# A store in a top-2 dispatch kernel moves from the sync queue to the scalar queue

## The chip, the cores and the metric

The kernel runs on one core of a Trainium2 chip. The metric is the time of the whole program on the device, in microseconds; the time given for a kernel is the median of its runs. A core has several engines with a queue of instructions each. Here only three matter: VectorE (DVE in the profile) does the arithmetic, the sync engine (SP) issues nearly all memory transfers (DMAs), and ScalarE (ACT) computes two sigmoids and issues one transfer. The transfers of all queues are carried out by the same 16 DMA engines. SBUF is the on-chip memory with 128 partitions; inputs and outputs lie in HBM.

## The reference

```python
batch, seq, hidden, n_experts, k = 16, 1024, 512, 8, 2

def reference(x, router_logits, k):
    logits_max = np.max(router_logits, axis=-1, keepdims=True)
    probs = np.exp(router_logits - logits_max)
    probs = probs / np.sum(probs, axis=-1, keepdims=True)
    topk_indices = np.argsort(probs, axis=-1)[..., -k:]
    topk_probs = np.take_along_axis(probs, topk_indices, axis=-1)
    topk_probs = topk_probs / np.sum(topk_probs, axis=-1, keepdims=True)
    x_expanded = x[:, :, np.newaxis, :].repeat(k, axis=2)
    return (x_expanded * topk_probs[..., np.newaxis]).astype(np.float32)
```

For each of the 16,384 tokens, the two largest of eight router logits are found, their softmax weights are normalised to a sum of 1, and the token's row of 512 floats is written out twice, once with each weight, the smaller first. The weights depend only on the difference of the two logits. So 33.6 MB of `x` are read and 67.1 MB are written.

## The kernel before

The 16,384 rows are spread over 128 partitions, 128 rows to a partition, in two groups of 65 and 63 rows per partition (`GROUPS`, L49). Within a group each partition has consecutive rows of HBM, so a transfer of n rows is one contiguous run of n x 2 KB per partition for a load, and n x 4 KB for a store.

Three buffers live through the whole program, with one copy each: `logits`, `xs` with room for 65 rows of `x` per partition, and `osp` with room for 16 rows of output (two scaled copies of a row each).

For each group the program first writes down the loads, all on the sync queue (L112): pieces of 2, 4, 2, 8, 17, 28 and 4 rows in the first group, and of 16, 16 and 31 rows in the second (`LOADS`, L51). In the first group, after 6 rows, the two loads of the logits follow, and `top2_weights` computes all the weights `WA` on VectorE, with two sigmoids on ScalarE.

Then comes a plan of products and stores. For each entry (first row, number of rows, target) VectorE multiplies the rows of `xs` by the two weights, in one instruction (L128), and the result is stored (L136). Targets are either `osp` (all 16 rows of it, or its halves of 8 rows) or, with `over`, a place inside `xs` whose rows have been used. In the second group the plan is: rows 0 to 15 into all of `osp`; rows 16 to 31 over `xs` rows 0 to 31; rows 32 to 39 into the first half of `osp`; rows 40 to 47 into its second half; rows 48 to 62 over `xs` rows 33 to 62. The buffers set the waits: the third and the fourth product write into `osp`, so they wait until the first store has read all of it. They also read rows that come with the last load of the group, the one of 31 rows (rows 32 to 62). The second group's loads in turn wait for the stores of the first group that read from `xs`.

Each queue takes its instructions in the order in which the program writes them. An issue on the sync queue waits in that queue for its data: a store for its product, a load for its room in `xs`. The store's queue is chosen in L135: the scalar queue if the piece has `e` = 2 rows, which is the first piece of the first group alone, and otherwise the sync queue. In this program `n` is the number of rows of the piece, `r` its first row and `g` the group.

Of the kernel before, what the change touches and what calls it, by code (L numbers as in the profile page):

```python
# [1 line left out]

# [4 lines left out]

F32 = mybir.dt.float32
ALU = mybir.AluOpType
ACTF = mybir.ActivationFunctionType  # L10
P = 128


def top2_weights(nc, pool, logits, M, E, tag=""):

    hi, lo, n = None, None, E  # L20
    while n > 1:
        n //= 2
        if hi is None:
            a, b = logits[:, :, 0:n], logits[:, :, n : 2 * n]
            nhi = pool.tile([P, M, n], F32, tag=f"hi{n}{tag}")
            nlo = b
            nc.vector.tensor_tensor(nhi, a, b, op=ALU.max)  # L27
            nc.vector.tensor_tensor(nlo, a, b, op=ALU.min)  # L28
        else:
            a, b = hi[:, :, 0:n], hi[:, :, n : 2 * n]  # L30
            nhi = pool.tile([P, M, n], F32, tag=f"hi{n}{tag}")
            nlo = pool.tile([P, M, n], F32, tag=f"lo{n}{tag}")
            tmp = pool.tile([P, M, n], F32, tag=f"tmp{n}{tag}")
            nc.vector.tensor_tensor(tmp, lo[:, :, 0:n], lo[:, :, n : 2 * n], op=ALU.max)  # L34
            nc.vector.tensor_tensor(nlo, a, b, op=ALU.min)  # L35
            nc.vector.tensor_tensor(nlo, nlo, tmp, op=ALU.max)  # L36
            nc.vector.tensor_tensor(nhi, a, b, op=ALU.max)  # L37
        hi, lo = nhi, nlo
    dlt = pool.tile([P, M], F32, tag=f"dlt{tag}")
    nc.vector.tensor_tensor(dlt, hi[:, :, 0], lo[:, :, 0], op=ALU.subtract)  # L40
    WA = pool.tile([P, M, 2], F32, tag=f"WA{tag}")
    nc.scalar.activation(WA[:, :, 0], dlt, ACTF.Sigmoid, scale=-1.0)  # L42
    nc.scalar.activation(WA[:, :, 1], dlt, ACTF.Sigmoid, scale=1.0)  # L43
    return WA

GROUPS = [65, 63]  # L49

LOADS = [[2, 4, 2, 8, 17, 28, 4], [16, 16, 31]]  # L51


LAST = [[(48, 9), (57, 8)], [(48, 15)]]


@with_exitstack
def kernel(
    ctx: ExitStack,
    tc: tile.TileContext,  # L60
    x: bass.AP,
    router_logits: bass.AP,
    k: bass.AP,
    out: bass.AP,
):
    nc = tc.nc
    B, S, D = x.shape
    E = router_logits.shape[-1]
    N = B * S
    assert int(k) == 2 and E == 8 and N == P * sum(GROUPS)  # L70
    M = N // P

    L = 16
    x_v, o_v, rl_v = [], [], []
    t0 = 0
    for n in GROUPS:
        t1 = t0 + P * n
        x_v.append(
            x.rearrange("b s d -> (b s) d")[t0:t1].rearrange("(p m) d -> p m d", p=P)
        )  # L80
        o_v.append(
            out.rearrange("b s k d -> (b s) k d")[t0:t1].rearrange(
                "(p m) k d -> p m k d", p=P
            )
        )
        rl_v.append(
            router_logits.rearrange("b s e -> (b s) e")[t0:t1].rearrange(
                "(p m) e -> p m e", p=P
            )
        )  # L90
        t0 = t1

    wpool = ctx.enter_context(tc.tile_pool(name="wpool", bufs=1))
    logits = wpool.tile([P, M, E], F32)
    xs = wpool.tile([P, max(GROUPS), D], F32)
    osp = wpool.tile([P, L, 2, D], F32)

    def over(r, n, G):

        a = 2 * r - G
        return xs[:, a : a + 2 * n, :].rearrange("p (r k) d -> p r k d", k=2)

    h = L // 2
    e = 2
    m0 = 0
    for g, G in enumerate(GROUPS):
        r = 0  # L110
        for n in LOADS[g]:
            nc.sync.dma_start(xs[:, r : r + n, :], x_v[g][:, r : r + n, :])  # L112
            r += n
            if g == 0 and r == 6:

                nc.sync.dma_start(logits[:, :G], rl_v[0])  # L116
                nc.sync.dma_start(logits[:, G:], rl_v[1])
                WA = top2_weights(nc, wpool, logits, M, E)
        assert r == G
        begin = [(0, e, osp[:, :e]), (e, L - e, osp[:, e:])] if g == 0 else [(0, L, osp)]  # L120
        plan = begin + [
            (L, L, over(L, L, 2 * L)),
            (2 * L, h, osp[:, :h]),
            (2 * L + h, h, osp[:, h:]),
        ]
        plan += [(r, n, over(r, n, G)) for r, n in LAST[g]]
        for r, n, og in plan:
            nc.vector.tensor_tensor(  # L128
                og,
                xs[:, r : r + n, :].unsqueeze(2).to_broadcast([P, n, 2, D]),  # L130
                WA[:, m0 + r : m0 + r + n, :].unsqueeze(3).to_broadcast([P, n, 2, D]),
                op=ALU.mult,
            )

            queue = nc.scalar if n == e else nc.sync  # L135
            queue.dma_start(o_v[g][:, r : r + n], og)  # L136
        m0 += G


# [1 line left out]
_INS = ['x', 'router_logits', 'k']  # L141
_OUTS = [((16, 1024, 2, 512), 'float32')]

_NUMBERS = {'k': 2}


# [26 lines left out]
```

## Time and profile before

| | |
|---|---|
| time, median of 3 runs | 240.18 us (240.09 to 240.56) |
| span of the profiled execution (it has no time of its own beside the span) | 238.6 us |
| VectorE busy | 142.0 us, 60% of the span |
| ScalarE busy | 1.8 us |
| bytes read from HBM / written to HBM | 34.08 MB / 67.11 MB |
| mean rate of the transfers over the span | 424 GB/s |
| VectorE waits for loads of `xs` | 31.1 us, once |
| VectorE waits for stores from `osp` | 30.2 us, twice, the longer 16.6 us |

The span runs from the first to the last instruction of one profiled execution. In the transfers' lines, q1 is the sync queue and q10 the scalar queue; their columns are packets, MB, and the time that the packets took as a share of 16 engines' time in the stretch asked for. A packet is counted in the stretch in which it starts, with its whole length, so that a short stretch can show more than 100%. In the lines of transfers by issue, the last number is the time from issue to landing, that is, until the transfer has signalled its completion; the KB, where a line has them, are the size of the transfer (the stores of 16 rows, 8192 KB, are shown without). In lines of waits and chains, SPq, ACTq and DVEq are the engines' sequencers, which issue transfers and wait on semaphores. `out_dram<-osp` is a store from `osp`, `out_dram<-xs` a store from inside `xs`, `xs<-in_x_dram` a load.

### The profile page before, as it was taken

Reading aid. Unit: us, or ns where it says so; the run is one execution under the profiler, and the core shown is the slowest. Engines: PE = TensorE matmul, PEld = TensorE weight load, DVE = VectorE, ACT = ScalarE, POOL = GpSimd, SP = SyncE. Lnnn points to the kernel's source line nnn. Section 1 sums busy time; section 2 is a strip of 40 time slices with the busy share of each in tenths; the row PEclk is TensorE's granted clock in tenths of the full one; section 3 lists DMA queues with packets and bytes.
Section 4 is the critical chain, followed back from the end, with each engine's and each line's share of the span. In section 5 each row is a group of like instructions: output and inputs, shape, how many; then the busy total and the mean of one; then the engine's idle time right before and its main releaser. Section 6 shows DMA issues by size and latency. Waiting matters only on the chain.

```text
span 238.6 us, 117 instructions
## 1 busy us (share of the span) xinstructions
DVE 142.0 (60%) x23; ACT 1.8 (1%) x3; POOL 0.2 (0%) x4
## 2 busy tenths in 40 slices
DVE  0589999900299699900000799999006999990000
ACT  2000000000000000000000000000000000000000
POOL 0000000000000000000000000000000000000000
DMA  7999999899898999999999999898999999999994
GB/s 260 435 470 404 422 493 462 330 462 462 374 484 352 440 440 440 440 433 446 440 434 434 429 456 479 373 495 374 484 396 462 418 407 396 429 440 429 495 474 185
DMA packets 3456, 101.19 MB, mean 424 GB/s; under 512 B 384, under 2 KB 512, under 8 KB 896
## 3 DMA queue, kind: packets, MB, share of 16 engines
q1 hardware_dynamic: 3312, 100.14, 97.7%
q10 hardware_dynamic: 144, 1.05, 1.0%
HBM read 34.08 MB, written 67.11 MB: 424 GB/s over the span
## 4 chain that ended last, share of the span: by engine, by line
DMA 43%; DVE 41%; issue 4%; SPq 1%; ACT 0%; DVEq 0%
DVE xs L128 22%; DVE osp L128 18%; DMA out_dram<-xs 15%; DMA out_dram<-osp 13%; DMA xs<-in_x_dram 13%; DMA logits<-in_router_logits_dram 3%; SPq L112 0%; DVE nhi L27 0%; DVE logits L28 0%; DVE nlo L36 0%; DVE nhi L37 0%; DVE nlo L35 0%; DVE tmp L34 0%; SPq L116 0%; SPq L136 0%
## 5 line engine op out<-in xcount | busy, mean ns | idle before, releaser
L128 DVE TENSOR_TENSOR osp<-xs,WA 128x8192 f32<-128x8192 f32 (+3 forms) x7 | 69.1, 9908 | 61.9 <-DMA xs<-in_x_dram 31.1
L128 DVE TENSOR_TENSOR xs<-xs,WA 128x16384 f32<-128x16384 f32 (+3 forms) x5 | 69.1, 13812 | 2.2 <-DMA out_dram<-xs 2.1
L27 DVE TENSOR_TENSOR nhi<-logits 128x512 f32<-128x512 f32 x1 | 0.7, 691 | 8.4 <-DMA logits<-in_router_logits_dram 8.4
L42 ACT ACT_TABLE_LOAD x1 | 1.3, 1283 | 0.7 <-PEq L154 0.7
L28 DVE TENSOR_TENSOR logits<-logits 128x512 f32<-128x512 f32 x1 | 0.7, 693 | 0.0
L37 DVE TENSOR_TENSOR nhi<-nhi 128x256 f32<-128x256 f32 (+1 forms) x2 | 0.7, 352 | 0.0
L35 DVE TENSOR_TENSOR nlo<-nhi 128x256 f32<-128x256 f32 (+1 forms) x2 | 0.7, 352 | 0.0
L36 DVE TENSOR_TENSOR nlo<-nlo,tmp 128x256 f32<-128x256 f32 (+1 forms) x2 | 0.7, 351 | 0.0
L34 DVE TENSOR_TENSOR tmp<-logits 128x256 f32<-128x256 f32 x1 | 0.4, 418 | 0.0
L42 ACT ACTIVATE WA<-dlt 128x128 f32<-128x128 f32 x1 | 0.3, 315 | 10.3 <-DVE dlt L40 10.3
L40 DVE TENSOR_TENSOR dlt<-nhi,nlo 128x128 f32<-128x128 f32 x1 | 0.3, 291 | 0.0
L43 ACT ACTIVATE WA<-dlt 128x128 f32<-128x128 f32 x1 | 0.3, 298 | 0.0
L34 DVE TENSOR_TENSOR tmp<-nlo 128x128 f32<-128x128 f32 x1 | 0.3, 284 | 0.0
L154 POOL MEMSET const-bfloat16-1.0<- 128x1 bf16 x1 | 0.1, 101 | 0.0
L154 POOL MEMSET const-uint8-127<- 128x1 uint8 x1 | 0.1, 101 | 0.0
L154 POOL MEMSET const-float32-0.0<- 128x1 f32 x1 | 0.1, 98 | 0.2 <-issue 0.2
L154 POOL MEMSET const-float32-1.0<- 128x1 f32 x1 | 0.1, 98 | 0.0
## 6 DMA issues: line engine op xcount, KB each, us to landing
out_dram<-osp SPq DMA_DIRECT2D x4, 4096.0 KB, 20.7
xs<-in_x_dram SPq DMA_DIRECT2D x2, 4096.0 KB, 29.9
xs<-in_x_dram SPq DMA_DIRECT2D x1, 7936.0 KB, 38.1
out_dram<-xs SPq DMA_DIRECT2D x1, 7680.0 KB, 23.2
xs<-in_x_dram SPq DMA_DIRECT2D x1, 7168.0 KB, 39.6
out_dram<-osp SPq DMA_DIRECT2D x1, 7168.0 KB, 33.8
out_dram<-xs SPq DMA_DIRECT2D x1, 4608.0 KB, 20.3
xs<-in_x_dram SPq DMA_DIRECT2D x1, 4352.0 KB, 22.7
```

The source lines that it names most:

```text
L27: nc.vector.tensor_tensor(nhi, a, b, op=ALU.max)
L28: nc.vector.tensor_tensor(nlo, a, b, op=ALU.min)
L34: nc.vector.tensor_tensor(tmp, lo[:, :, 0:n], lo[:, :, n : 2 * n], op=ALU.max)
L35: nc.vector.tensor_tensor(nlo, a, b, op=ALU.min)
L36: nc.vector.tensor_tensor(nlo, nlo, tmp, op=ALU.max)
L37: nc.vector.tensor_tensor(nhi, a, b, op=ALU.max)
L40: nc.vector.tensor_tensor(dlt, hi[:, :, 0], lo[:, :, 0], op=ALU.subtract)
L42: nc.scalar.activation(WA[:, :, 0], dlt, ACTF.Sigmoid, scale=-1.0)
L43: nc.scalar.activation(WA[:, :, 1], dlt, ACTF.Sigmoid, scale=1.0)
L128: nc.vector.tensor_tensor(og, xs[:, r : r + n, :].unsqueeze(2).to_broadcast([P, n, 2, D]), WA[:, m0 + r : m0 + r + n, :].unsqueeze(3).to_b ...
L154: nc = _bacc.Bacc("TRN2", target_bir_lowering=False, num_devices=1)
```

## The change

The condition that chooses a store's queue gets a second case: the first store of the second group (`g == 1 and r == 0`, 16 rows of each partition, from `osp`) is issued by ScalarE's sequencer and goes over the scalar queue. The loads, the products, the sizes and all other stores stay as they are, in the same order.

```diff
-            queue = nc.scalar if n == e else nc.sync
+            queue = nc.scalar if n == e or (g == 1 and r == 0) else nc.sync
             queue.dma_start(o_v[g][:, r : r + n], og)
```

## The prediction

> **What bounds the kernel now.** The page's head, its DMA totals and its queues come first.
>
> ```profile
> span 238.6 us, 117 instructions
> ...
> DMA packets 3456, 101.19 MB, mean 424 GB/s; under 512 B 384, under 2 KB 512, under 8 KB 896
> ...
> q1 hardware_dynamic: 3312, 100.14, 97.7%
> q10 hardware_dynamic: 144, 1.05, 1.0%
> ```
>
> The transfer engines are full nearly all the time, and nearly all of it comes from the sync queue (q1). The scalar queue (q10) carries one store, the 2 rows of the first group. The 24 transfers of the program make 24 x 128 packets, one for each partition's whole run, and 24 x 16 = 384 tiny ones that signal completion: so each of the 16 engines has 8 data packets and one signal packet in a transfer. Next the chain of waits in order of time, over the second group; columns are start, length, what.
>
> ```profile
> 102.28 30.65 DMA xs<-in_x_dram
> ...
> 132.95 17.24 DVE osp L128
> 150.19 0.02 issue
> 150.21 30.76 DMA out_dram<-osp
> ...
> 189.67 8.70 DVE osp L128
> 198.37 0.02 issue
> 198.39 16.16 DVE xs L128
> ```
>
> VectorE's last three products (8, 8 and 15 rows) can't begin before the moved store, S1 from here, has let go of `osp`: S1 is issued at 150.21 and lands at 180.97. The third view is the time from issue to landing, by transfers, in stretches around each issue.
>
> ```profile
> xs<-in_x_dram SPq DMA_DIRECT2D x1, 7936.0 KB, 38.1
> ...
> out_dram<-osp SPq DMA_DIRECT2D x1, 30.8
> ...
> out_dram<-xs SPq DMA_DIRECT2D x1, 32.8
> ...
> out_dram<-osp SPq DMA_DIRECT2D x1, 4096.0 KB, 21.3
> ...
> out_dram<-xs SPq DMA_DIRECT2D x1, 7680.0 KB, 23.2
> ```
>
> In order: the last load, issued 123.5, lands 161.6; S1 lands 181.0; the second store S2, issued 167.47, lands 200.3; the fourth, S4, issued 198.4, lands 219.7; the last, S5, issued 214.57, lands 237.8. S1 takes 19.4 us after the load and S2 19.3 us after S1: the sync queue works them off one after the other. Two facts set the sum. First, S5 waits in line: of the 29 packets that start between 218 and 219, 14 are S4's signals (under 512 B) and the rest are nearly all S5's first data, so S5 starts at about 218.7, though it was issued at 214.57. An idle queue starts sooner (the first load is issued at 0.73, its first packet starts at 1.73), so S5 could have started at 215.6. VectorE's chain therefore has 3.1 us of slack. Second, nothing idles that a new queue could fill: from 142 to 161 the engines move 436 GB/s.
>
> **The change, part by part.** It adds no instruction, no byte and no arithmetic. S1's issue goes from the sync sequencer (0.34 us at 150.21) to the scalar one, where the only row shows 0.37 us. ScalarE has done its last work at 12.9 us and its queue holds nothing else, so the issue waits for nothing new; the sync sequencer, waiting for VectorE at that time, gains nothing but a free 0.34 us. Both count as nothing. If ScalarE had work there, the cost would be that work. S1's one DMA moves past what remains of the last load, and gets S2, formerly behind it, as a competitor. That order is the whole effect, so the question is how two queues share an engine. The 2-row store on the scalar queue is the row that answers, at stretches 27 to 29, 31.5 to 34 and 34 to 36 us (packets started, MB, share):
>
> ```profile
> 15.20 0.37 ACTq L136 DMA_DIRECT2D out_dram<-osp  x1
> ...
> q1 hardware_dynamic: 16, 0.92, 105.8%
> q10 hardware_dynamic: 16, 0.13, 15.4%
> ...
> q1 hardware_dynamic: 16, 0.92, 84.6%
> q10 hardware_dynamic: 16, 0.06, 5.6%
> ...
> q1 hardware_dynamic: 16, 0.92, 105.8%
> q10 hardware_dynamic: 7, 0.00, 0.2%
> ```
>
> One packet of each queue on each engine, in turn, whatever their sizes: 57 KB of the load against 8 KB of the store. That is why 1.05 MB needed 20.3 us. Three details matter. The first store packet starts at 18.6, after two load packets that began once the issue was made (16.2, 17.4). The pair takes 2.42 us, the 2.1 of the load's packet plus 0.3 of the store's, so reading and writing don't overlap. And the completion signal takes a turn too: 9 engines signal in 31.5 to 34 and 7 in 34 to 36, after one more load packet each.
>
> The Trainium skill ("DMA: Bandwidth & Descriptors", "Queues, rings and completion order") has the engine alternate between queues by packets of typically 9 to 17 descriptors. By that, the load's 8 pieces on an engine would be one turn, S1 would start after them as before, and the time would be 240.2. The trace's strict one-for-one turns by single partition runs say otherwise. The same page ("Issuing engines are not separate DMA queues") holds that a second issuing engine saves issue time only, again 240.2; the 20.3 us of that small store show that order changes as well.
>
> Now S1's landing. A load packet (31 rows, 62 KB) takes 2.3 us, a 64 KB store packet 2.42 us (19.4 / 8). The load's fourth packet starts at 149.0; the fifth and sixth (151.3, 153.5) go first, as two did for the small store. From 155.8 on: two load packets 4.6, S1's eight 19.4, and S2's packets that get in between. Up to 170.0 they are S1 1, load 7, S1 2, load 8, S1 3, the load's signal, S1 4. S2 is issued at 167.47; with the same start delay S1's fifth goes before it, to 172.5. Then S2 1, S1 6, S2 2, S1 7, S2 3, S1 8, S2 4, signal: four S2 packets, 9.7 us. 155.8 + 4.6 + 19.4 + 9.7 = 189.5, and about 1.0 for the signal to land (its packets start near 180.0 before, the landing is 180.97): **190.5**, 9.5 later than before. How many load packets go first doesn't matter, since all eight are through by 168 either way.
>
> From there VectorE is as before: 214.57 - 180.97 = 33.6 us from landing to S5's issue, so 224.1. All earlier stores are through by about 221 (S3 is issued at 199.3, S4 at 208.0, 9.7 us each), so S5 meets idle engines: first packet 1.0 us later at 225.1, and 19.1 us more (218.7 to 237.8) to its landing at 244.2. The same by slack: 9.5 - 3.1 = +6.4 us. What the load now lands later, about 168.5 for 161.6, is hidden behind S1's wait. The span of 238.6 becomes 245.0; the median shown, 240.18, is 1.58 us above that span (the profiled execution has no time of its own beside it), taken as unchanged: **246.6**.
>
> Unknown costs. S2's start: one packet of S2 more or less before S1's end is 2.42 us (small-store rows: two packets went first on some engines, three on others), so 244.2 to 249.0; the slowest engine decides, and I take the middle. S5's start on idle engines: 1.0 us from the first load, at most 3.4 from the small store into full queues, so up to +2.4; I take 1.0, the row with idle engines. Sharing could cost rate: the small store's stage moved 6.8 MB from 18.6 to 34.7, 424 GB/s against 436, 3% of the 34 us of sharing, 1 us; I take 0 and leave the 1 us to the range.
>
> **Rivals.** That the change doesn't do what it says is out: the load's packets start from 142.4 on and it lands at 161.6, so it is in flight when S1 is issued at 150.2. *S1 is served ahead or whole (no change).* If the scalar queue had precedence, S1 would land at about 175, but the load at 181.0, and the product of rows 32 to 39 needs that load: VectorE resumes at 181 all the same, 240.2. So too if S1, once started, keeps S2 out until done. Anything that lands S1 by 184.1 costs nothing, the slack being 3.1. Against it: the one-for-one turns. Chance 0.07.
> *The two directions overlap (faster).* If load packets 7 and 8 ran beside S1's, 4.6 us of transfer would vanish; S1, still sharing with S2, would land near 181, and S5 would start when VectorE is done, 215.6 for 218.7: 3.1 us less, 237.1. It wins from S1 landing before 184.1 together with engines that free up early. Against it: 2.1 + 0.3 = 2.42, no overlap seen. Chance 0.04.
> *S1 gets less than half (worse).* If S2's queue has two turns to S1's one, four more S2 packets would precede the end, but only eight exist: +9.7, 256.3; with one or two more, 249.0 to 251.5. For it: uneven engines. Chance 0.09.
>
> **How the numbers follow.** Forecast 0.80, its own range 244.2 to 249.0. The range given, 243.6 to 249.5, adds the start of S5 and the rate, and leaves out the rivals' 0.20 but for the edge of the last. This kernel can be told from no change at about 0.2%, 0.5 us. Faster 0.04, same 0.07, slower 0.89.
>
> **What would show it.** Right: q10 carries 9.4 MB; the last load lands near 168 to 170; from 172 on, q1 and q10 start equal numbers of packets; S1 lands near 190 and the wait of VectorE on `osp` there grows from 13.6 to about 23 us; the DMA row shows a gap of about 5 us before S5. Wrong: S1 lands by 184, or S5 still finds a line before it, or S1's packets come in a row after 170.

## The result, and the profile after

The changed kernel takes 246.38 us (median of 5 runs), the kernel before 240.18 us: a ratio of 1.0253, 95% interval 1.0233 to 1.0272. It is slower by 6.2 us. The one profiled execution of that set took 250.72 us where its four other runs took 246.25 to 246.54, so the profile after that is shown here is the one of the same kernel run once more (first experiment; 246.31 us, span 244.5).

First the page of that profile: its head, the DMA totals, the two queues, and the group of the products into `osp`.

```profile
span 244.5 us, 118 instructions
...
DMA packets 3456, 101.19 MB, mean 414 GB/s; under 512 B 384, under 2 KB 512, under 8 KB 896
...
q1 hardware_dynamic: 3168, 91.75, 87.6%
q10 hardware_dynamic: 288, 9.44, 8.9%
...
L128 DVE TENSOR_TENSOR osp<-xs,WA 128x8192 f32<-128x8192 f32 (+3 forms) x7 | 69.1, 9908 | 71.5 <-DMA out_dram<-osp 39.8
```

The work is the same: the same packets and bytes, the same 69.1 us in this group. (The one instruction more, 118 for 117, is a semaphore instruction in ScalarE's queue.) 8.39 MB have moved from q1 to q10. The idle time before the group has grown from 61.9 us, as the page of the kernel before has it, to 71.5:

```profile
L128 DVE TENSOR_TENSOR osp<-xs,WA 128x8192 f32<-128x8192 f32 (+3 forms) x7 | 69.1, 9908 | 61.9 <-DMA xs<-in_x_dram 31.1
```

The releaser named for most of it is now a store from `osp` (39.8 us in all, 30.2 before). Next the same execution's chain of waits in order of time; columns are start, length, what.

```profile
150.29 40.30 DMA out_dram<-osp
...
190.69 0.10 DVE osp L128
190.78 8.51 issue
199.29 8.69 DVE osp L128
207.99 0.02 issue
208.01 16.16 DVE xs L128
```

The store S1 lands 40.30 us after its issue, at 190.59, where it took 30.76 before. Everything on VectorE after it is unchanged in length, so the whole chain is 9.6 us later. The third view counts the packets of both queues that start in short stretches of the same execution: 172 to 174, 175 to 176, 177 to 179, 180 to 181, 186 to 188 and 189 to 191 us.

```profile
q1 hardware_dynamic: 16, 1.05, 120.9%
...
q10 hardware_dynamic: 16, 1.05, 241.8%
...
q1 hardware_dynamic: 16, 1.05, 120.9%
...
q10 hardware_dynamic: 16, 1.05, 241.8%
...
q1 hardware_dynamic: 16, 1.05, 120.9%
...
q1 hardware_dynamic: 16, 1.05, 120.9%
q10 hardware_dynamic: 16, 0.00, 0.5%
```

This is the loss, seen directly: on all 16 engines one packet of the second store S2 (q1), one of S1 (q10), and so on; 182 to 184 and 184 to 186 us, not shown, go on in the same way with 16 packets of q1 and 16 of q10. The line for 186 to 188 is S2's fourth packet on each engine. Only behind it, in the last pair of lines, do S1's 16 tiny signal packets start, together with S2's fifth. The fourth view is DMA share and GB/s (the last two columns) at the end of this execution.

```profile
216.00:219.10 3.10, 3.10 (x1) 0.00 (x0) 0.00 (x0) 1.00 1.18 507
219.10:225.00 5.90, 5.07 (x1) 0.00 (x0) 0.00 (x0) 1.00 0.00 0
225.00:243.00 18.00, 0.00 (x0) 0.00 (x0) 0.00 (x0) 1.00 1.01 437
```

The delay comes out at the end as 5.9 us in which the engines move nothing: VectorE is busy with the last product, and the last store, S5, isn't issued before 224.20.

### The profile page after: what moved, and what is told of

Read it like the earlier page. It is cut to its first block, busy times and chain, and to the rows that moved or that the text cites. A ratio compares the mean times of both kernels' runs of the same rounds, so it can differ in the third digit from the quotient of the medians.

```text
span 248.9 us, 118 instructions
## 1 busy us (share of the span) xinstructions
DVE 142.0 (57%) x23; ACT 1.8 (1%) x3; POOL 0.2 (0%) x4
## 4 chain that ended last, share of the span: by engine, by line
DMA 47%; DVE 40%; issue 4%; SPq 1%; ACT 0%; DVEq 0%
DVE xs L128 21%; DMA out_dram<-osp 18%; DVE osp L128 17%; DMA out_dram<-xs 15%; DMA xs<-in_x_dram 12%; DMA logits<-in_router_logits_dram 3%; SPq L112 0%; DVE nhi L27 0%; DVE logits L28 0%; DVE nlo L36 0%; DVE nhi L37 0%; DVE nlo L35 0%; DVE tmp L34 0%; SPq L116 0%; SPq L136 0%
## 5 line engine op out<-in xcount | busy, mean ns | idle before, releaser
L128 DVE TENSOR_TENSOR osp<-xs,WA 128x8192 f32<-128x8192 f32 (+3 forms) x7 | 69.1, 9908 | 75.7 <-DMA out_dram<-osp 44.1
L128 DVE TENSOR_TENSOR xs<-xs,WA 128x16384 f32<-128x16384 f32 (+3 forms) x5 | 69.1, 13811 | 2.2 <-DMA out_dram<-xs 2.1
## 6 DMA issues: line engine op xcount, KB each, us to landing
out_dram<-xs SPq DMA_DIRECT2D x1, 7680.0 KB, 19.5
```

The lines of the kernel that those rows point to most:

```text
L128: nc.vector.tensor_tensor(og, xs[:, r : r + n, :].unsqueeze(2).to_broadcast([P, n, 2, D]), WA[:, m0 + r : m0 + r + n, :].unsqueeze(3).to_b ...
```

## The experiments

Three theories stood against each other. *Turns*: S2 enters on the other queue and takes every second turn from S1. *The load*: S1 is late because it now shares with the last load. *The queue*: large transfers on the scalar queue are slow in themselves.

**e1: the change once more.** No edit.

> The changed kernel as it is, for a trace of an ordinary execution. Theory (turns): the second store S2 enters on the sync queue while S1 runs on the scalar queue, the engines serve one packet of each in turn, S1 lands near 190.5 (about 40 us after its issue), VectorE's last three products start 9.5 us later, the last store S5 meets idle engines: 246.4 us, span about 244.6. Rival (the load): S1 is late because it shares with the last load: then its packets start equal numbers with the load's and it lands late even though S2's packets come after it. Rival (the queue): packets on the scalar queue are themselves slower, more than 2.42 us each.

Measured: 246.36 us (ratio 1.0249, 1.023 to 1.0269), span 244.5, S1 landed at 190.59. At the end S1's packets alternate with S2's and not with the load's, and a packet takes 2.42 us on either queue (above, 241.8% of a stretch of 1 us for S1's, 120.9% of 2 us for S2's): a packet on the scalar queue is no slower. This speaks for turns and against the queue; the load is left to the next two.

**e2: S2 follows S1 to the scalar queue.**

```diff
-            queue = nc.scalar if n == e or (g == 1 and r == 0) else nc.sync
+            queue = nc.scalar if n == e or (g == 1 and r <= L) else nc.sync
```

> S1 and S2 both on the scalar queue, so that S2 stays behind S1 in one queue while S1 still shares with the load. Theory (turns): nothing cuts in after the load, S1 ends after 155.8 + 4.6 + 19.4 = 179.8 and lands at about 180.8, inside the slack: 240.2 us, no change against before (within 0.5). Rival (the load): the sharing with the load is still there: 246.4. Rival (the queue): two large stores on the scalar queue: 246.4 or more.

Measured: 240.37 us, ratio 1.0007 (0.9996 to 1.0018). First its chain of waits, then the packets that start in 156 to 157, 172 to 174 and 175 to 176 us.

```profile
150.16 30.82 DMA out_dram<-osp
```

```profile
q1 hardware_dynamic: 8, 0.51, 124.4%
q10 hardware_dynamic: 8, 0.52, 120.9%
...
q10 hardware_dynamic: 16, 1.05, 120.9%
...
q10 hardware_dynamic: 16, 1.05, 241.8%
```

The sharing with the load is there (half of the engines serve the load, half S1), and the load lands at 171.1, 47.5 us after its issue. Yet S1 lands at 180.99 as in the kernel before, because from 172 on there is nothing but q10. The whole loss is gone with S1 still on the scalar queue and still beside the load. The load and the queue both fall.

**e3: S2 alone on the scalar queue, S1 on the sync queue as before.**

```diff
-            queue = nc.scalar if n == e or (g == 1 and r == 0) else nc.sync
+            queue = nc.scalar if n == e or (g == 1 and r == L) else nc.sync
```

> S1 on the sync queue behind the load as before, S2 alone on the scalar queue. Theory (turns): S1 starts at 160.7 and has the engines to itself until S2 enters after its fifth packet at about 172.7; four packets of S2 get in before S1's signal: S1 lands at about 190.5, 246.4 us (244 to 249). Rival (the load): S1 shares nothing with the load: 240.2. Rival (the queue): S1 is not on the scalar queue, 240.2, or a little more if S2 itself is late.

Measured: 246.12 us, ratio 1.024 (1.0221 to 1.0259). Its chain of waits:

```profile
150.26 40.36 DMA out_dram<-osp
...
190.72 0.10 DVE osp L128
```

Here S1 shares nothing with the load and isn't on the scalar queue, and it lands at 190.62, as late as in the change. So, with both stores whole, what matters is that S1 and S2 are on different queues, whichever of them is moved.

**e4: the change, with S2 in four stores of 4 rows.**

```diff
+            step = 4 if g == 1 and r == L else n
+            for c in range(0, n, step):
+                queue.dma_start(o_v[g][:, r + c : r + c + step], og[:, c : c + step])
-            queue.dma_start(o_v[g][:, r : r + n], og)
```

> As the change, but S2 is issued as four stores of 4 rows each on the sync queue: same bytes, packets of 16 KB (0.61 us) in place of 64 KB (2.42 us). Theory (one packet each in turn, whatever the size): four turns of S2 take 2.4 us in place of 9.7, S1 lands at about 183.2, just inside the slack that ends at 184.1: 240.2 us, at most 241.5. Rival (the engines share by bytes): S1 lands at 190.5 as in the change, 246.4.

Measured: 240.65 us, ratio 1.0017 (1.0006 to 1.0028). Its chain of waits, and its last store with the time from issue to landing:

```profile
150.85 32.95 DMA out_dram<-osp
```

```profile
out_dram<-xs SPq DMA_DIRECT2D x1, 7680.0 KB, 20.8
```

S1 took 32.95 us against the 33.0 that 183.2 - 150.21 asks for. S5 still had a short line before it (20.8 us; on idle engines it is 19.5, see e5). Turns by packet are right, sharing by bytes (246.4) is wrong. The time is 0.5 above before, at the edge of what can be told; in the profiled execution (240.95 us) the stage itself began 0.64 us later than before, ahead of anything that differs. Whether the median's 0.5 has the same cause stays open.

**e5: the change, with S2 in two stores of 8 rows** (`step = 8` in the diff above).

> As the change, with S2 as two stores of 8 rows: packets of 32 KB, 1.21 us. Theory (one packet each in turn): four turns of S2 take 4.8 us in place of 9.7, S1 lands at about 185.7, 4.7 us later than before; the slack takes 3.1 of it: +1.6, 241.8 us (241.3 to 242.3). Rival (share by bytes): 246.4. Rival (no slack, VectorE's delay counts in full): 244.9.

Measured: 241.6 us, ratio 1.0056 (1.0043 to 1.0069), against 240.28 for the kernel before in this set: +1.3. Its chain of waits, the DMA share and GB/s around the last store's issue, and the time of that store from issue to landing:

```profile
150.23 35.58 DMA out_dram<-osp
```

```profile
216.00:218.50 2.50, 2.50 (x1) 0.00 (x0) 0.00 (x0) 1.00 0.97 419
218.50:220.20 1.70, 0.89 (x1) 0.00 (x0) 0.00 (x0) 1.00 0.01 0
```

```profile
out_dram<-xs SPq DMA_DIRECT2D x1, 7680.0 KB, 19.5
```

S1 landed at 185.81 (185.7 was expected). 4.8 us of delay become 1.3 us of time, and the engines move next to nothing for 1.7 us before S5. This is what a slack does, and excludes that VectorE's delay counts in full (244.9).

**e6: the change, with S1 in four stores of 4 rows.** The loop of e4, with `r == 0` in place of `r == L`.

> As the change, with S1 as four stores of 4 rows on the scalar queue (packets of 16 KB, 0.61 us) and S2 whole on the sync queue. Theory (one packet each in turn, whatever the size): the small packets of S1 each wait for a 64 KB packet of S2; the first two parts land by about 177, so rows 32 to 39 are computed early and S3 is queued early, but the last part lands only near 208 to 211, the fourth product starts there, S5 is issued at about 233 to 235 and the time is 253 to 258 us. Rival (the engines share by bytes): S1's last part lands at 190.5 or earlier, 246.4 or less.

Measured: 258.78 us, ratio 1.0755 (1.0729 to 1.0781), a little above the range of 253 to 258. The packets that start in 174 to 176 us, and those in 209 to 213:

```profile
q1 hardware_dynamic: 16, 1.05, 120.9%
q10 hardware_dynamic: 16, 0.26, 30.6%
...
DMA packets 20, 0.05 MB, mean 12 GB/s; under 512 B 17, under 2 KB 17, under 8 KB 17
q10 hardware_dynamic: 4, 0.05, 2.9%
```

and the third and the fourth product, in its timeline (start, length, shape, idle time before it):

```profile
177.72 8.69 DVE L128 TENSOR_TENSOR osp<-xs,WA 128x8192 f32<-128x8192 f32 x1 [9.90 <-DMA out_dram<-osp]
...
211.60 8.69 DVE L128 TENSOR_TENSOR osp<-xs,WA 128x8192 f32<-128x8192 f32 x1 [25.19 <-DMA out_dram<-osp]
```

One for one again: 16 packets of 16 KB for 16 of 64 KB, so the queue with the small packets gets a fifth of the bytes (0.26 of 1.31 MB). The third product needs only S1's first two parts and starts at 177.72, earlier than in any other version; the fourth pays for it. The same 8.39 MB on the same queue now let go of the rest of `osp` only at 211.50. Of the 20 packets started in 209 to 213, four are S1's, three with data and one signal: 15 of its last signals had started by 209, the sixteenth waited until after 211, and VectorE waits for all sixteen. Without that one engine the part would have landed some 2 us earlier, as an estimate, inside the 208 to 211 that was expected; why that engine was behind stays open.

## Why the prediction was right

246.6 us was predicted, 246.38 measured. The mechanism came as forecast, but that the number is within 0.3 us is in part luck: the span was forecast as 245.0 and is 244.5, because the slack was put too low (below), while the 1.58 us from span to time were too few: in the runs on record that give both, the time is about 1.8 us above the span (246.31 for 244.5 here), so the profiled execution before (238.6) was one of about 240.4. The two errors go against each other. By its steps:

- *The issue costs nothing on either queue.* S1 was issued at 150.29 by ScalarE's sequencer in 0.34 us, 0.08 later than before, and S2 at 167.54 for 167.47. Right.
- *One packet each in turn, whatever the size.* Right in e1, and tested from both sides: with S2's packets at a quarter (e4) S1 took 2.2 us longer than before, at a half (e5) 4.8, whole 9.5, and with S1's own packets at a quarter (e6) its last part landed 30 us after S1 before. The Trainium skill's rule in "DMA: Bandwidth & Descriptors", "Queues, rings and completion order", turns of typically 9 to 17 descriptors, gives 240.2 for the change if a descriptor is taken to be one partition's run, as the prediction took it. The traces show turns of a single run, and 246.38; how many descriptors a run has they don't show.
- *S1's start on the other queue doesn't matter.* Four of the engines took S1's first packet at 153 to 155, the others after 155; the prediction had 155.8 for all. All had started five packets of S1 by 172.
- *Four packets of S2 get in before S1's signal; S1 lands at 190.5.* Measured 190.59. S2 entered on all engines in 172 to 174 (172.5 predicted), after S1's fifth packet there, and its fourth in 186 to 188.
- *The late load is hidden.* It landed at 171.2 (123.55 + 47.7) where about 168.5 was expected: on four engines its signal took its turn only after 170. S1's wait covered that with 19 us to spare. In e2, where that wait is shorter, the load lands at 171.1 and still costs nothing.
- *Sharing costs no rate.* The prediction took 0 and left 1 us to the range, from 6.8 MB at 424 GB/s beside the small store; the trace has 6.95 MB there, 431 GB/s. In e2, S1 and the load share the engines and S1 lands at 180.99, in 180.97 before: 0 was right.
- *Slack of 3.1 us, S5 on idle engines.* The mechanism was right, the size a little small. S5 was issued at 224.20 (224.1 predicted) and landed 19.5 us later, where 1.0 + 19.1 = 20.1 was predicted: its first packets started after about 0.85 us, and with all engines starting together the transfer took 18.65. So the slack is about 3.7: S5's issue 9.63 later than before, its landing, 243.7 for 237.77, 5.9 later. e5 gives the same: issue 4.85 later, landing 1.15 later.
- *The rivals.* "Served ahead or whole" would have kept S2 out until S1 was done; four of its packets got in on every engine. Where S2 is kept out, in e2, the time is indeed 240.37. "The directions overlap" would have shown S1 landing near 181; it didn't. "S1 gets less than half" by turns didn't happen at equal packet sizes; in e6 it did by bytes.

That the change removes a wait of S1 behind the load was true and worth nothing: the product that follows needs the load as well as S1. With both whole and the engines full, one of the two ends near 181 in any order; this is argued from the bytes, and e2, with both in flight at once, agrees (S1 at 180.99). Only a part of S1 can come earlier: in e6, with S1 in four, VectorE went on at 177.72, and lost far more at the next product. No version here beats the kernel before.

## What to carry to other kernels

A queue is also an order. In this kernel, splitting two stores over two queues gave up that order, and whoever is released by the first transfer pays for the packets of the second that now get in between: keep what VectorE waits for and what was queued behind it on the same queue, or give the later one small packets. When the engines are full already, ask of such a move not what starts earlier but what lands later, and take off the time for which the last transfer would have stood in line anyway.

## What was not expected of the hardware

The prediction had read the turns from one small store; how much they are worth is what the experiments add. In these runs shares go by packet, where a packet is one partition's contiguous run: 16 KB runs beside 64 KB runs got a fifth of the engines (e6: 0.26 of 1.31 MB in a stretch), and splitting a store, with its bytes and queue unchanged, moved the kernel's time from 246.4 to 258.8 us or, on the competitor's side, to 240.65. The completion signal takes a turn of its own, too: in e1 S1's signals started in 189 to 191, after a further packet of S2, though its last data packets had started by 186.
